# A sparse-expert encoder layer on one core: small experts in two passes with rows and rests side by side, and each weight tile split by one cast and one subtraction

## The chip, the cores and the metric

The kernel runs on one core of a Trainium2 chip. The metric is the device time of one execution in microseconds (us). Before the change the median of three runs was 1533.52 us (1529.77 to 1535.05).

## The reference, cut to what matters

One layer over 1024 tokens of width 1024: a conditioned norm, one projection into a convolution, a neighbourhood attention and a gated delta-rule mixer, an output projection, a second norm, and then a mixture of 32 experts (4 groups of 8, two experts per token). All of it is float32. The change lies in the experts:

```python
def expert_block(args):
    xb, e = args
    return (jax.nn.silu(xb @ w1[e]) * (xb @ w3[e])) @ w2[e]
```

Each expert has `w1` and `w3` of 1024 x 512 and `w2` of 512 x 1024. The result is scaled by the token's gate and added to the token. There are 2048 (token, expert) pairs; how many fall on an expert depends on the router.

## The kernel before, in words

The mixers and the router come first and end at about 870 us. From then on the kernel goes through 32 positions, one expert each (L1546). Positions 0 to 2 hold experts 0 to 2; the others hold the remaining experts by size, found by `by_size` (L1294) on the chip. `column(p)` (L1204) maps a position to a column of that order: positions 18 and 24 hold the two largest (columns 3 and 4), the rest follow in order of size. `ROOM` (L30) gives the rows kept for a column: 128 for the first three, 192 for the two largest, and then 128, 96, 80, 64 and 48. A room of 192 makes two blocks, one of 128 rows and a rest of 64 (`late`, L1548). A loop at L1611 runs once for every 128 rows that did not find room; its instructions are not in this trace.

**One expert.** The weights of an expert are six tiles of 1 MB, 128 partitions x 4 x 512 float32: two of `w1`, two of `w3`, two of `w2`. SP loads them (`load_tile`, L1175) into 16 buffers (`WA` 5, `WX` 3, `WB` 8, L1161); `weights` (L1528) takes the oldest and asks for the next, and a load waits for the one four before it (`FLY`, L1162). TensorE multiplies in a rounded format (F32R), so a float32 operand is cut into a rounded part and a rest: `split` (L60) casts on ScalarE (`wh`) and subtracts on VectorE (`wl`). `chunk_split` (L1268) cuts a weight tile into two halves of 1024 columns, each with its own `wh` and `wl`, from a pool `exw` of three buffers each (L1266). The first four tiles are split in pieces of 512.

**One block** (`class Block`, L1359). `gather` fetches the rows, `x` transposes them (eight transposes, L1378) and splits them into `xh` and `xl`. `hidden` (L1504) makes `h1` and `h3`: for each of four weight tiles, `mm3` (L1351) multiplies three passes, (`xh`,`wh`), (`xl`,`wh`), (`xh`,`wl`), with the rows as the stationary operand and 512 weight columns moving: 12 matmuls per tile, whatever the number of rows. `gated` (L1382) makes `u` = silu(h1) * h3, `t` (L1389) transposes `u` (four transposes) and splits it into `uh` and `ul`, and `y` (L1399) makes the output from two tiles in three passes and scales it into `yo`; `out` adds `yo` to the residual by an indirect DMA.

**Order.** In the program position p does: `hidden(p)`, `x` of the block of p + 1, `output(p - 1)`, `t(p)`. The weight tiles are used strictly in that order. The order on each engine is made from it when the kernel is built; each engine then works through its own list in order, and semaphores hold it where a buffer or an operand is missing. A buffer of a pool goes to the next tile when the last instruction that uses the old one has ended.

The last two blocks are not scattered; their rows are added to the residual on the chip (`last`, L1584), which ends in the final norm and the stores.

Of the kernel before, what the change touches and what calls it, by code (L numbers as in the profile page):

```python
# [16 lines left out]
P = 128  # L17
# [3 lines left out]
KT = D // P  # L21
# [5 lines left out]
TWICE = (18, 24)  # L27
LATE = 5
FEATS = (*range(0, 1280, P), *range(1536, 3072, P))
ROOM = ((3, 128), (5, 192), (12, 128), (16, 96), (20, 80), (27, 64), (32, 48))  # L30


def body(tc, I, O):
# [5 lines left out]
def _body(ctx, tc, nc, I, O):  # L39
# [1118 lines left out]
        yield  # L1158

    VS = 2  # L1160
    WA, WX, WB = 5, 3, 8  # L1161
    FLY = 4  # L1162
    arrived = mybir.DependencyInfo(mybir.DependencyClass.Sync, mybir.DependencyReason.DATA)
    loaded, used, loads, flying = [], [0], [0], []
# [98 lines left out]
        dve.tensor_scalar(v, tv, 0.0, 1e6, op0=OP.is_equal, op1=OP.mult)  # L1263
        dve.scalar_tensor_tensor(ix_, tv, -1.0, v, op0=OP.add, op1=OP.add)

    exw = ctx.enter_context(tc.tile_pool(name="exw", bufs=3))  # L1266

    def chunk_split(w, n=1):  # L1268

        parts = []  # L1270
        for k0 in (0, 2):
            wh = exw.tile([P, 2, 512], F32R, name="wh")
            wl = exw.tile([P, 2, 512], F32R, name="wl")
            for k in range(0, 2, 2 // n):
                split(*(x[:, k:k + 2 // n] for x in (wh, wl, w[:, k0:k0 + 2])))
            parts.append((wh, wl))
        return parts

    indices(mo, tab[:, 0], ix, E)
    gp = tab[:, 1]  # L1280
# [70 lines left out]
    def mm3(out, xh, xl, k0, w, first, last):  # L1351
        n = 0
        for k in range(4):
            wh, wl = w[k // 2]
            for a, b in ((xh, wh), (xl, wh), (xh, wl)):
                pe.matmul(out, a[:, k0 + k], b[:, k % 2], start=first and n == 0, stop=last and n == 11)  # L1356
                n += 1

    class Block:  # L1359


        def __init__(self, i, idx, n=P):
            self.n = n
            self.xg, self.idx, self.yo = xgs[i % 3][:n], lambda: [x[:n] for x in idx()], None

        def gather(self):
            return pool.indirect_dma_start(out=self.xg, out_offset=None, in_=xn_d,  # L1367
# [2 lines left out]

        def x(self):
            n = self.n
            xh = ex.tile([P, KT, P], F32R, name="xh")[:, :, :n]
            xl = ex.tile([P, KT, P], F32R, name="xl")[:, :, :n]
            for g in range(2):
                pt = pse.tile([P, 4, P], F32, name="pt", bufs=2)[:, :, :n]
                for j in range(4):
                    pe.transpose(pt[:, j], self.xg[:, (4 * g + j) * P:(4 * g + j + 1) * P], ident[:n, :n])  # L1378
                split(xh[:, 4 * g:4 * g + 4], xl[:, 4 * g:4 * g + 4], pt)
            self.xs = xh, xl  # L1380

        def gated(self, n):  # L1382
            if n:
                self.yo = ex.tile([P, D], F32, name="yo", bufs=2)[:self.n]
            u = self.u = self.yo[:, :512] if n else ex.tile([P, 512], F32, name="u", bufs=1)[:self.n]
            act.activation(u, self.hs[0], AF.Silu)
            dve.tensor_mul(u, self.hs[1], u)

        def t(self, n=0):  # L1389
            m = self.n  # L1390
            pt = pse.tile([P, 4, P], F32, name="ut")[:, :, :m]
            for j in range(4):
                pe.transpose(pt[:, j], self.u[:, j * P:(j + 1) * P], ident[:m, :m])
            uh = ex.tile([P, 4, P >> n], F32R, name=f"uh{n}", bufs=1)[:, :, :m]
            ul = ex.tile([P, 4, P >> n], F32R, name=f"ul{n}", bufs=1)[:, :, :m]
            split(uh, ul, pt)
            self.us = uh, ul
# [41 lines left out]
    def slots_of(ebs, ob):  # L1439


        m = len(ebs)
        pb = ex.tile([P, 2, NT], F32, name="pb", bufs=1)
        dve.tensor_scalar(pb, pos, ob, None, op0=OP.add)
        sl = ex.tile([P, NT, 2, 2, 2], F32, name="sl", bufs=1)[:, :, :, :m]
        on = ex.tile([P, NT, 2], F32, name="on", bufs=1)
        for i, eb in enumerate(ebs):
            dve.tensor_scalar(on, eid, eb, None, op0=OP.is_equal)
            dve.tensor_mul(sl[:, :, :, i], slot, on[:, :, :, None].to_broadcast([P, NT, 2, 2]))
        tabo = pse.tile([P, 512], F32, name="tab")[:, :2 * m]  # L1450
        n = 0
        for t in range(NT):
            for a in range(2):
                q = ex.tile([P, P], F32, name="q", bufs=1)
                dve.tensor_scalar(q, iota, pb[:, a, t:t + 1], None, op0=OP.is_equal)
                pe.matmul(tabo, q, sl[:, t, a].rearrange("p i k -> p (i k)"), start=n == 0, stop=n == 2 * NT - 1)
                n += 1
        tb = small.tile([P, 2, 2], F32, name="tb")[:, :m]
        dve.tensor_copy(tb, tabo.rearrange("p (i k) -> p i k", k=2))
        ix1 = small.tile([P, 2], I32, name="ix1")[:, :m]  # L1460
        indices(small, tb[:, :, 0], ix1, m)
        return [(ix1[:, i:i + 1], tb[:, i, 1:2], tb[:, i, 0:1]) for i in range(m)]
# [41 lines left out]
    def hidden(bs, weights, between=iter(())):  # L1504

        for b in bs:
            b.hs = []
        for nms in (("h1", "tab"), ("h3", "y")):
            for b, nm in zip(bs, nms):
                b.hs.append(pse.tile([P, 512], F32, name=nm, bufs=2 if nm == "y" else 1)[:b.n])  # L1510
            for g in range(2):
                next(between, None)
                w = weights()
                for b in bs:
                    mm3(b.hs[-1], *b.xs, 4 * g, w, g == 0, g == 1)
        for n, b in enumerate(bs):
            b.gated(n)

# [7 lines left out]
                b.out()  # L1526

    def weights():  # L1528
        w = chunk_split(loaded.pop(0), 2 if used[0] < 4 else 1)
        used[0] += 1  # L1530
        owed[0] += 1
        while owed[0] and len(loaded) + used[0] < len(loading) and (
# [346 lines left out]
```

## Time and profile before

| | |
|---|---|
| median of the runs | 1533.52 us |
| the profiled execution, its own time | 1529.12 us |
| its span (first to last instruction) | 1527.3 us |
| mean granted TensorE clock | 0.967 |
| TensorE matmul busy | 1380.7 us (90%) |
| VectorE busy | 1185.0 us (78%) |
| ScalarE busy | 792.4 us (52%) |
| GpSimd busy | 380.9 us (25%) |
| largest DMA queue | 351.13 MB |

Line numbers (L61) are those of the kernel before. PE is TensorE's matmuls, PEld its weight loads, DVE VectorE, ACT ScalarE, POOL GpSimd, SP the engine that issues most DMAs. A group is named by its line, its engine and its operands, output first: `h<-wh,xl` is a matmul into `h` with `wh` moving and `xl` stationary. Busy time of the matmuls counts overlapped ones once; their ends are modelled. A clock of 1.00 is 2.4 GHz.

### The profile page before, as it was taken

How to read it: one execution, taken by the hardware profiler on the slowest of the kernel's cores; microseconds unless marked ns; L12 is line 12 of the kernel's file. 1: busy time of each engine (PE TensorE's matmuls, PEld its weight loads, DVE VectorE, ACT ScalarE, POOL GpSimd, SP SyncE). 2: the span in 40 equal slices, each digit the busy share in tenths (PEclk: the TensorE clock that was granted, in tenths of full speed). 3: DMA queues.
4: the chain of work that ended last, by engine and by line, in shares of the span. 5: the costliest groups of instructions: out<-in, count | busy, mean ns of one | idle time of the engine just before them, and what ended most of it. 6: DMA issues, size and time to landing. Idle time of an engine off the chain costs nothing. (4 is left out here: it accounts for less than half of the span.)

```text
span 1527.3 us, 21968 instructions
## 1 busy us (share of the span) xinstructions
PE 1380.7 (90%) x7319; PEld 1054.2 (69%) x7319; DVE 1185.0 (78%) x2148; ACT 792.4 (52%) x1293; POOL 380.9 (25%) x294
## 2 busy tenths in 40 slices
PE   3987999999877898879999699999999999999994
PEld 3865777777665888878887578787766665665542
DVE  6758766554647688867788799999999789878995
ACT  3633554433444322322322288787777567657773
POOL 0011321100101555633432111221244113212222
PEclk9999999999999999999999599999999999999997
DMA  9496455224778665677566699999999999979832
GB/s 338 120 200 195 143 183 165 88 75 96 204 208 208 187 202 181 203 252 238 207 207 226 255 335 374 346 381 364 351 374 370 363 337 371 334 271 339 322 111 117
DMA packets 172601, 375.75 MB, mean 246 GB/s; under 512 B 33458, under 2 KB 99634, under 8 KB 147908
## 3 DMA queue, kind: packets, MB, share of 16 engines
q1 hardware_dynamic: 162500, 351.13, 67.2%
q0 software_dynamic: 7072, 16.73, 4.6%
q10 hardware_dynamic: 2912, 6.46, 1.4%
q8 instruction: 59, 0.97, 0.3%
q14 instruction: 58, 0.48, 0.1%
HBM read 325.31 MB, written 56.87 MB: 250 GB/s over the span
## 5 line engine op out<-in xcount | busy, mean ns | idle before, releaser
L61 DVE TENSOR_TENSOR wl<-w,wh 128x1024 fp32r<-128x1024 f32 (+1 forms) x392 | 460.6, 1196 | 44.8 <-ACT wh L61 39.7
L61 ACT CAST wh<-w 128x1024 fp32r<-128x1024 f32 (+1 forms) x392 | 403.9, 1033 | 161.2 <-PE y L1356 69.1
L1356 PE MATMUL h<-wl,xh 128*128 128x512 f32 (+4 forms) x512 | 204.1, 399 | 0.4 <-DVE wl L61 0.3
L1356 PE MATMUL h<-wh,xh 128*128 128x512 f32 (+4 forms) x512 | 204.4, 399 | 0.1
L1356 PE MATMUL h<-wh,xl 128*128 128x512 f32 (+4 forms) x512 | 202.0, 394 | 0.6 <-DVE xl L61 0.6
L1408 POOL DMA_INDIRECT x_d<-yo,ixp x27 | 100.0, 3703 | 198.6 <-DVE yo L1404 184.1
L339 PE MATMUL mm<-hh,wh 128*128 128x512 f32 x352 | 148.1, 421 | 0.0
L339 PE MATMUL mm<-hh,wl 128*128 128x512 f32 x352 | 143.0, 406 | 1.9 <-DVE wl L61 1.9
L339 PE MATMUL mm<-hl,wh 128*128 128x512 f32 x352 | 142.6, 405 | 0.0
L1356 PE MATMUL y<-wh,uh 128*128 128x512 f32 (+4 forms) x272 | 108.8, 401 | 1.1 <-ACT uh L61 1.1
L1356 PE MATMUL y<-wl,uh 128*128 128x512 f32 (+4 forms) x272 | 108.1, 398 | 0.1
L1356 PE MATMUL y<-wh,ul 128*128 128x512 f32 (+4 forms) x272 | 106.9, 394 | 0.5 <-DVE ul L61 0.5
L1356 PEld LDWEIGHTS h<-wl,xh 128*128 128x128 f32 (+4 forms) x512 | 80.9, 158 | 36.8 <-DVE wl L61 2.0
L1356 PEld LDWEIGHTS h<-wh,xl 128*128 128x128 f32 (+4 forms) x512 | 81.0, 158 | 36.7 <-DVE xl L61 1.4
L1356 PEld LDWEIGHTS h<-wh,xh 128*128 128x128 f32 (+4 forms) x512 | 81.1, 158 | 34.2 <-ACT wh L61 0.7
L1367 POOL DMA_INDIRECT oacc<-xn_d,ixp x29 | 35.2, 1213 | 211.4 <-PE pt L1378 195.5
L339 PEld LDWEIGHTS mm<-hh,wh 128*128 128x128 f32 x352 | 68.1, 193 | 18.5 <-issue 7.0
L339 PEld LDWEIGHTS mm<-hl,wh 128*128 128x128 f32 x352 | 67.7, 192 | 15.5 <-issue 0.3
L339 PEld LDWEIGHTS mm<-hh,wl 128*128 128x128 f32 x352 | 68.1, 193 | 13.9 <-DVE wl L61 2.2
L404 POOL TENSOR_TENSOR acc<-acc,wa 128x512 f32<-128x512 f32 x28 | 41.1, 1466 | 86.3 <-ACT wa L402 47.8
L1356 PEld LDWEIGHTS y<-wl,uh 128*128 128x128 f32 (+4 forms) x272 | 42.5, 156 | 21.2 <-DVE wl L61 2.2
L1356 PEld LDWEIGHTS y<-wh,uh 128*128 128x128 f32 (+4 forms) x272 | 42.4, 156 | 19.4 <-ACT uh L61 1.6
(433 smaller groups left out, 2893.3 us busy)
## 6 DMA issues: line engine op xcount, KB each, us to landing
w<-we SPq DMA_DIRECT2D x192, 1024.0 KB
wa<-w_ada SPq DMA_DIRECT2D x64, 256.0 KB
wa<-w_ada SPq DMA_DIRECT2D x16, 512.0 KB
wr<-w_in_f SPq DMA_DIRECT2D x16, 512.0 KB
qkv_d<-t SPq DMA_DIRECT2D x12, 512.0 KB
f<-qkv_d SPq DMA_DIRECT2D x8, 768.0 KB
t_d<-zt SPq DMA_DIRECT2D x8, 516.0 KB
xt<-x SPq DMA_DIRECT2D x8, 512.0 KB
```

The source lines that it names most:

```text
L61: return act.copy(hi, src), dve.tensor_sub(lo, src, hi.bitcast(F32))
L339: pe.matmul(ps, a[:, k], of(b, k, h * 512, 512), start=n == 0, stop=n == 3 * KT - 1)
L404: pool.tensor_add(acc, acc, w)
L1356: pe.matmul(out, a[:, k0 + k], b[:, k % 2], start=first and n == 0, stop=last and n == 11)
L1367: return pool.indirect_dma_start(out=self.xg, out_offset=None, in_=xn_d, in_offset=bass.IndirectOffsetOnAxis(ap=self.idx()[0], axis=0), bo ...
L1408: return pool.indirect_dma_start(out=x2_d, out_offset=bass.IndirectOffsetOnAxis(ap=self.idx()[0], axis=0), in_=self.yo, in_offset=None, bo ...
```

## The change

Small experts (a room of 64 or less) put the rounded rows and their rests side by side in one stationary operand of 128 columns, so that two passes (`wh`, `wl`) do for the hidden part: partitions 0 to 63 of `h` hold the products of the rounded rows, 64 to 127 those of the rests. A matrix `fold` (two identities of 64) then adds the two halves while it transposes; Silu and the product follow after the transposition. The output keeps three passes. `ROOM` has two sizes behind the two largest experts, 128 up to column 13 and 64 from there on. `chunk_split` splits a whole tile by one cast and one subtraction, into two buffers in place of three half ones; the first four tiles still go in pieces of 512. The weight tiles have 15 buffers in place of 16. The scratch `q` of `slots_of` uses the buffer of `u`.

```diff
--- before.py
+++ after.py
@@ -27,7 +27,8 @@
 TWICE = (18, 24)
 LATE = 5
 FEATS = (*range(0, 1280, P), *range(1536, 3072, P))
-ROOM = ((3, 128), (5, 192), (12, 128), (16, 96), (20, 80), (27, 64), (32, 48))
+ROOM = ((3, 128), (5, 192), (14, 128), (32, 64))
+HALF = P // 2
 
 
 def body(tc, I, O):
@@ -1158,7 +1159,7 @@
         yield
 
     VS = 2
-    WA, WX, WB = 5, 3, 8
+    WA, WX, WB = 4, 3, 8
     FLY = 4
     arrived = mybir.DependencyInfo(mybir.DependencyClass.Sync, mybir.DependencyReason.DATA)
     loaded, used, loads, flying = [], [0], [0], []
@@ -1263,18 +1264,15 @@
         dve.tensor_scalar(v, tv, 0.0, 1e6, op0=OP.is_equal, op1=OP.mult)
         dve.scalar_tensor_tensor(ix_, tv, -1.0, v, op0=OP.add, op1=OP.add)
 
-    exw = ctx.enter_context(tc.tile_pool(name="exw", bufs=3))
+    exw = ctx.enter_context(tc.tile_pool(name="exw", bufs=2))
 
     def chunk_split(w, n=1):
 
-        parts = []
-        for k0 in (0, 2):
-            wh = exw.tile([P, 2, 512], F32R, name="wh")
-            wl = exw.tile([P, 2, 512], F32R, name="wl")
-            for k in range(0, 2, 2 // n):
-                split(*(x[:, k:k + 2 // n] for x in (wh, wl, w[:, k0:k0 + 2])))
-            parts.append((wh, wl))
-        return parts
+        wh = exw.tile([P, 4, 512], F32R, name="wh")
+        wl = exw.tile([P, 4, 512], F32R, name="wl")
+        for k in range(0, 4, 4 // n):
+            split(*(x[:, k:k + 4 // n] for x in (wh, wl, w)))
+        return [(wh[:, k:k + 2], wl[:, k:k + 2]) for k in (0, 2)]
 
     indices(mo, tab[:, 0], ix, E)
     gp = tab[:, 1]
@@ -1356,12 +1354,25 @@
                 pe.matmul(out, a[:, k0 + k], b[:, k % 2], start=first and n == 0, stop=last and n == 11)
                 n += 1
 
+    fold = ex.tile([P, HALF], F32, name="fold", bufs=1)
+    dve.tensor_add(fold, ident[:, :HALF], ident[:, HALF:])
+
+    def mm2(out, xs, k0, w, first, last):
+
+        n = 0
+        for k in range(4):
+            for b in w[k // 2]:
+                pe.matmul(out, xs[:, k0 + k], b[:, k % 2], start=first and n == 0, stop=last and n == 7)
+                n += 1
+
     class Block:
+
 
 
         def __init__(self, i, idx, n=P):
             self.n = n
             self.xg, self.idx, self.yo = xgs[i % 3][:n], lambda: [x[:n] for x in idx()], None
+            self.both = n <= HALF
 
         def gather(self):
             return pool.indirect_dma_start(out=self.xg, out_offset=None, in_=xn_d,
@@ -1370,16 +1381,28 @@
 
         def x(self):
             n = self.n
-            xh = ex.tile([P, KT, P], F32R, name="xh")[:, :, :n]
-            xl = ex.tile([P, KT, P], F32R, name="xl")[:, :, :n]
+            xh = ex.tile([P, KT, P], F32R, name="xh")
+            if self.both:
+                self.xs = xh
+                xh, xl = xh[:, :, :n], xh[:, :, HALF:HALF + n]
+            else:
+                xh, xl = xh[:, :, :n], ex.tile([P, KT, P], F32R, name="xl")[:, :, :n]
+                self.xs = xh, xl
             for g in range(2):
                 pt = pse.tile([P, 4, P], F32, name="pt", bufs=2)[:, :, :n]
                 for j in range(4):
                     pe.transpose(pt[:, j], self.xg[:, (4 * g + j) * P:(4 * g + j + 1) * P], ident[:n, :n])
                 split(xh[:, 4 * g:4 * g + 4], xl[:, 4 * g:4 * g + 4], pt)
-            self.xs = xh, xl
+
+        def hidden(self, w, g):
+            (mm2 if self.both else mm3)(self.hs[-1], *((self.xs,) if self.both else self.xs), 4 * g, w, g == 0, g == 1)
 
         def gated(self, n):
+            if self.both:
+                self.hc = ex.tile([P, KT, P], F32, name="xl").rearrange("p (i k) f -> p i k f", i=2)
+                for i in range(2):
+                    act.copy(self.hc[:, i].rearrange("p k f -> p (k f)"), self.hs[i])
+                return
             if n:
                 self.yo = ex.tile([P, D], F32, name="yo", bufs=2)[:self.n]
             u = self.u = self.yo[:, :512] if n else ex.tile([P, 512], F32, name="u", bufs=1)[:self.n]
@@ -1388,9 +1411,20 @@
 
         def t(self, n=0):
             m = self.n
-            pt = pse.tile([P, 4, P], F32, name="ut")[:, :, :m]
-            for j in range(4):
-                pe.transpose(pt[:, j], self.u[:, j * P:(j + 1) * P], ident[:m, :m])
+            pt = pse.tile([P, 4, P], F32, name="ut")
+            if self.both:
+                ht = pt.rearrange("p k (i f) -> p i k f", i=2)
+                for i in range(2):
+                    for j in range(4):
+                        pe.matmul(ht[:, i, j], self.hc[:, i, j], fold, start=True, stop=True)
+                su = ex.tile([P, 512], F32, name="u", bufs=1).rearrange("p (i k f) -> p i k f", i=2, k=4)
+                act.activation(su[:, 0], ht[:, 0], AF.Silu)
+                dve.tensor_mul(su[:, 1], ht[:, 1], su[:, 0])
+                pt = su[:, 1][:, :, :m]
+            else:
+                pt = pt[:, :, :m]
+                for j in range(4):
+                    pe.transpose(pt[:, j], self.u[:, j * P:(j + 1) * P], ident[:m, :m])
             uh = ex.tile([P, 4, P >> n], F32R, name=f"uh{n}", bufs=1)[:, :, :m]
             ul = ex.tile([P, 4, P >> n], F32R, name=f"ul{n}", bufs=1)[:, :, :m]
             split(uh, ul, pt)
@@ -1451,7 +1485,7 @@
         n = 0
         for t in range(NT):
             for a in range(2):
-                q = ex.tile([P, P], F32, name="q", bufs=1)
+                q = ex.tile([P, 512], F32, name="u", bufs=1)[:, :P]
                 dve.tensor_scalar(q, iota, pb[:, a, t:t + 1], None, op0=OP.is_equal)
                 pe.matmul(tabo, q, sl[:, t, a].rearrange("p i k -> p (i k)"), start=n == 0, stop=n == 2 * NT - 1)
                 n += 1
@@ -1507,12 +1541,12 @@
             b.hs = []
         for nms in (("h1", "tab"), ("h3", "y")):
             for b, nm in zip(bs, nms):
-                b.hs.append(pse.tile([P, 512], F32, name=nm, bufs=2 if nm == "y" else 1)[:b.n])
+                b.hs.append(pse.tile([P, 512], F32, name=nm, bufs=2 if nm == "y" else 1)[:P if b.both else b.n])
             for g in range(2):
                 next(between, None)
                 w = weights()
                 for b in bs:
-                    mm3(b.hs[-1], *b.xs, 4 * g, w, g == 0, g == 1)
+                    b.hidden(w, g)
         for n, b in enumerate(bs):
             b.gated(n)
 
@@ -1526,7 +1560,7 @@
                 b.out()
 
     def weights():
-        w = chunk_split(loaded.pop(0), 2 if used[0] < 4 else 1)
+        w = chunk_split(loaded.pop(0), 4 if used[0] < 4 else 1)
         used[0] += 1
         owed[0] += 1
         while owed[0] and len(loaded) + used[0] < len(loading) and (
```

## Rows read from the trace of the kernel before

**Rows 1.** The page: busy time of the engines, and the granted clock in 40 slices.
```profile
PE 1380.7 (90%) x7319; PEld 1054.2 (69%) x7319; DVE 1185.0 (78%) x2148; ACT 792.4 (52%) x1293; POOL 380.9 (25%) x294
...
PEclk9999999999999999999999599999999999999997
```

**Rows 2.** Busy time by windows of the expert stage; last: clock, DMA share, GB/s.
```profile
core 0: us, PE busy (x) PEld busy (x) DVE busy (x) ACT busy (x) POOL busy (x), PEclk, DMA share, GB/s
1040.00:1180.00 140.00, 139.98 (x665) 98.69 (x664) 136.60 (x143) 111.29 (x127) 43.93 (x16) 1.00 1.00 363
1380.00:1440.00 60.00, 60.00 (x276) 32.10 (x275) 54.82 (x58) 45.00 (x53) 17.59 (x6) 1.00 0.95 356
```

**Rows 3.** Waits from 880 to 1440 us: us in total, times, longest us.
```profile
ACT wh L61 <- PE y L1356: 61.5, 104, 3.2
ACT wh L61 <- PE h L1356: 59.3, 151, 1.5
```

**Rows 4.** Activations at L1386 in four windows: count, durations (ns), first and last start.
```profile
L1386 ACT ACTIVATE u<-h x11: 583/587/591, 894.3 to 1078.7; 128x512 f32<-128x512 f32 x9, 96x512 f32<-96x512 f32 x2
...
L1386 ACT ACTIVATE u<-h x7: 583/585/588, 1078.7 to 1184.9; 80x512 f32<-80x512 f32 x4, 96x512 f32<-96x512 f32 x3
...
L1386 ACT ACTIVATE u<-h x10: 582/586/597, 1184.9 to 1383.4; 64x512 f32<-64x512 f32 x7, 128x512 f32<-128x512 f32 x2, 80x512 f32<-80x512 f32 x1
...
L1386 ACT ACTIVATE u<-h x6: 579/584/587, 1383.4 to 1475.0; 48x512 f32<-48x512 f32 x5, 64x512 f32<-64x512 f32 x1
```

**Rows 5.** TensorE in order of time, 1405 to 1408 us: start, duration, instruction.
```profile
1406.23 0.40 PE L1356 MATMUL h<-wh,xh 128*48 128x512 f32 x1
1406.47 0.40 PE L1356 MATMUL h<-wh,xl 128*48 128x512 f32 x1
```

**Rows 6.** TensorE in order of time, 884 to 887 us: eight transposes.
```profile
885.31 1.03 PE L1378 MATMUL pt<-ident,oacc 128*128 128x128 f32 x8
```

**Rows 7.** Groups by form, 850 us to the end: busy us, mean ns, idle before.
```profile
L61 DVE TENSOR_TENSOR wl<-w,wh 128x1024 fp32r<-128x1024 f32 x376 | 450.0, 1218 | 43.8 <-ACT wh L61 38.9
L61 ACT CAST wh<-w 128x1024 fp32r<-128x1024 f32 x376 | 395.0, 1051 | 157.2 <-PE y L1356 69.1 <-PE h L1356 65.3 <-issue 8.0
...
L61 DVE TENSOR_TENSOR xl<-pt,xh 128x512 fp32r<-128x512 f32 x24 | 16.3, 684 | 0.8 <-ACT xh L61 0.6
...
L1404 DVE SCALAR_TENSOR_TENSOR yo<-y,tabp,oacc 128x512 f32<-128x512 f32 x18 | 13.5, 748 | 1.5 <-PE y L1356 1.4
...
L61 DVE TENSOR_TENSOR wl<-w,wh 128x512 fp32r<-128x512 f32 x16 | 10.7, 683 | 1.0 <-ACT wh L61 0.8
...
L61 DVE TENSOR_TENSOR xl<-pt,xh 128x256 fp32r<-128x256 f32 x18 | 7.0, 410 | 0.4 <-ACT xh L61 0.4
...
L61 ACT CAST wh<-w 128x512 fp32r<-128x512 f32 x16 | 8.9, 616 | 4.0 <-PE h L1356 2.8 <-PE pl L1020 1.2
```

**Rows 8.** ScalarE in order of time, around 1406 and 1490 us; idle before, and releaser.
```profile
1405.49 1.05 ACT L61 CAST wh<-w 128x1024 fp32r<-128x1024 f32 x1 [0.36 <-PE h L1356]
1406.90 1.05 ACT L61 CAST wh<-w 128x1024 fp32r<-128x1024 f32 x1 [0.36 <-PE h L1356]
...
1489.84 1.05 ACT L61 CAST wh<-w 128x1024 fp32r<-128x1024 f32 x1 [2.33 <-PE y L1356]
```

**Rows 9.** VectorE in order of time, around 1407 and 1488 us.
```profile
1406.57 1.23 DVE L61 TENSOR_TENSOR wl<-w,wh 128x1024 fp32r<-128x1024 f32 x1 [0.19 <-ACT wh L61]
...
1488.28 0.34 DVE L61 TENSOR_TENSOR ul<-ut,uh 128x192 fp32r<-128x192 f32 x1
```

**Rows 10.** TensorE in order of time, around 1489 us: a matmul that waited for a subtraction.
```profile
1488.68 0.43 PE L1356 MATMUL y<-wh,ul 128*48 128x512 f32 x1 [0.46 <-DVE ul L61]
```

**Rows 11.** SP's weight loads, 1040 to 1180 us and 1180 us on: first and last start.
```profile
L1178 SPq DMA_DIRECT2D w<-we x44: 332/333/342, 1041.9 to 1179.9; - x44
...
L1178 SPq DMA_DIRECT2D w<-we x80: 332/333/346, 1179.9 to 1441.7; - x80
```

**Rows 12.** Busy time and granted clock, 400 to 440 us (columns as in rows 2).
```profile
400.00:440.00 40.00, 31.51 (x166) 25.11 (x165) 19.73 (x41) 19.49 (x63) 5.42 (x4) 0.93 0.69 199
```

## The prediction

> **What bounds the kernel now.** I read the page first: TensorE is busy 90% of the span at a granted clock of 9 tenths or more in nearly every slice, VectorE 78% [rows 1]. These are means over different stages, and every edit lies in the expert stage (about 870 us to the end), so I took that by windows next. From 1040 to 1180 us the matmuls fill 139.98 of 140 us, VectorE 136.60, and the DMA engines 1.00 of their time [rows 2]: three resources are full together. The waits say which one ends last. The longest ones on ScalarE and VectorE are casts that wait for matmuls (`wh` waits for `y` and `h`, 255 times, 120.8 us) [rows 3]; TensorE waits for nothing of note. So TensorE sets the pace, and a cast starts when a matmul lets go of a `wh` buffer. The ScalarE activations at L1386, one per position, give the pace: position 1 to 11 take 184.4 us, 11 to 17 106.2, 17 to 26 198.5 (positions 18 and 24 have a rest beside them), 26 to 31 91.6 [rows 4]. That is 17.7 us for an undisturbed single position (106.2 / 6) and 18.3 for the last ones (91.6 / 5).
>
> **The change, part by part.**
>
> *Matmuls saved.* Matmuls of 512 columns start 0.23 to 0.24 us apart (the recorded 0.40 overlaps the next) [rows 5]; I use 0.23. A single position has 72 of them (16.6 us) and 12 transposes at 0.13 (eight take 1.03 us [rows 6]): 18.1 us at most, which is the measured pace. After, a 64-row block needs 8 instead of 12 for each of four hidden tiles, 56 in all. In 18 small positions and 2 rests that is 320 x 0.23 = 74 us less on TensorE. Whether the span gets them depends on what feeds TensorE.
>
> *Splits merged.* By form, a cast takes 616 ns for 512 elements and 1051 for 1024, a subtraction 683 and 1218 [rows 7]. The slopes, 0.85 and 1.045 ns per element, put a cast of 2048 at 1.92 us and a subtraction at 2.29; no row has this size, and the bounds are twice the short one (2.10, 2.44) and the bare slope (1.74, 2.14). Per tile VectorE saves 2 x 1.218 - 2.29 = 0.15 us, 29 us over 192 tiles.
>
> *Buffers.* This is the part that decides. Before, three half-tile slots: a slot is taken from the start of its cast to the last `wh` matmul of that half. Rows show each link: the last `wh` matmul of a half starts at 1406.47 and lasts 0.40 [rows 5], and the next cast starts at 1406.90 [rows 8], 0.03 later; the cast of 1405.49 ends at 1406.54 [rows 8] and its subtraction starts at 1406.57 [rows 9]; a subtraction that ends at 1488.62 lets its matmul go at 1488.68 [rows 9, 10], 0.06 later. From the first `wl` matmul of a half (its third) to its last `wh` matmul (its fifth) are 2 steps, so a slot turns round in 0.06 + 0.46 + 0.40 + 0.03 + 1.05 + 0.03 + 1.22 = 3.25 us, and three slots could deliver a tile (two halves) every 2.2 us; TensorE takes 2.95. Cover enough.
>
> After, two whole-tile slots. With three passes, from the third matmul to the eleventh are 8 steps: 0.06 + 1.84 + 0.40 + 0.03 + 1.92 + 0.03 + 2.29 = 6.57 us for a slot, so a tile every 3.29 us at best, though TensorE needs 2.76. With two passes the first `wl` matmul is the second and the last `wh` one the seventh, 5 steps: 5.88 us, a tile every 2.94, though TensorE needs 1.84. Each of the two slots serves three of the six tiles of a position: a 128-row position is 3 x 6.57 = 19.7 us, a small one (output keeps three passes) 2 x 5.88 + 6.57 = 18.3. The first is 2.0 us above today, and the small ones, for which the passes were cut, stay where they are: the cut passes turn into TensorE waiting for `wl`.
>
> *Positions.* The new ROOM makes positions 0 to 11 single 128-row blocks, 18 and 24 a 128-row block with a 64-row rest, and the other 18 small. Position 1 to 11: ten times 17.7 are 177 of the 184.4 us; the other 7.4 (start, and the slot lists of position 5) lie partly in the new stalls, I keep 4. So 197 + 4 = 201, +16.6; the hidden part of position 0, four tiles at up to 0.34 more (3.29 against 2.95), adds 1. Position 11 to 17: 6 x 18.33 = 110.0, +3.8. Position 17 to 26 is two groups of three intervals about a rest, and three single ones. In such a group the hidden tiles of 18 have 20 matmuls (4.6 us, over the slots' 4.2, so TensorE-bound), four of them 18.4; its output tiles, 24 matmuls each, take 11.0; the two other output pairs 6.6 each, two small hidden parts 11.8 each, and 1.5 for transposes in the bound parts: 67.7. Twice 67.7 and 3 x 18.33 are 190.4 against 198.5, -8.1. Position 26 to 31: 5 x 18.33 = 91.7, +0.1. Tail: the last splits are 4.2 us long instead of 2.3, and the chain fold, Silu, product, split before the last output has two operations more; +2, bounds 0 and +5. Together +15.4 us.
>
> *Operations that meet the chain.* A slot's turn holds only if ScalarE and VectorE are free at the moment. VectorE has, between subtractions, 3.29 - 2.29 = 1.0 us per tile, into which a position's six others must fit (`xl` 0.684 twice, `u` and `ul` of that size, `yo` 0.748 twice [rows 7]; 4.2 us, in a small position 3.1, with `xl` 0.41). One that comes ready late in the gap delays the subtraction by up to 0.4; the same holds for ScalarE's four casts and activations, and the 12 transposes (1.6 us) stand partly among the matmuls of the turn. Bounds: 0.3 us per position (all in gaps) and 2.0 (half of it in the way). I take 1.0, since before too some of them fall into VectorE's short gaps: 24 single intervals, +24 us (7 to 48).
>
> *Edits at no cost.* The fold: eight matmuls of 64 columns instead of four transposes, between 0.13 and 0.23 each, +0.5 to +1.3 us of TensorE per small position, where it now stands 18.3 - 12.9 - 1.0 = 4.4 us; without that cover, +1 us times 18. The two ScalarE copies of 128x512 replace an activation at about 0.6; ScalarE, 111.29 of 140 us busy [rows 2], keeps 1.3 us per tile. The product on VectorE shrinks from 512 columns to 256. One weight tile fewer ahead: SP issued 44 loads from 1041.9 to 1179.9, 3.21 us apart, with DMA full [rows 11, 2]. At 19.7 us per six tiles (3.29) loads keep up, so nothing; if the stage ran faster than 3.21 per tile this would be the next bound. `q` in `u`'s buffer stays one buffer as before and waits at one position, 0 to 3 us, within the 4 above.
>
> **Sum.** The profiled execution took 1529.1 us; + 15.4 + 24 = 1568.5. The median of the runs is 4.4 above the profiled one, so 1573 in their terms.
>
> **Rivals.**
> 1. *VectorE was the true limit and its relief counts.* VectorE is 97.6% busy from 1040 to 1180 [rows 2]. If waits for slots are only shadows of it, fewer operations and passes win: small positions go to VectorE's pace, 54.82 of 60 us busy [rows 2] x 18.3 = 16.7, less 0.9 for six splits and 0.3 for the product: 15.5. Then loads bound: the last is issued at 1441.7 [rows 11], at 3.21 us each from 1179.9 it would be 1433.5, landing some 13 later (four in flight), against a last cast at 1489.84 [rows 8]: -43, 1486, 1490 in the runs' terms. It decides from the point where cast and subtraction together fit beside one tile's matmuls, 3.2 us; they are 4.2. Against: TensorE itself is unbroken, and casts wait for matmuls, not for VectorE [rows 3]. The Trainium skill (Perfetto Trace Analysis, Optimizing Scalar/DVE Operations) says that larger operations raise throughput if the engine is saturated, which speaks for this rival; the same section says that breaking instructions up may finish work sooner where ScalarE and VectorE hold other engines up, which speaks for my sum. VectorE at 97.6% meets the first condition today, and the slot's turn makes the second one true after.
> 2. *The clock.* With stalls in every tile the granted clock may fall: 400 to 440 us had TensorE busy 31.51 of 40 and 0.93 granted [rows 12]. If the stage gets 0.90 (a fifth of the time at 1.2 GHz, where a step takes twice 0.23), the five steps of a turn cost 1.15 us more in that fifth, 3.5 per small position, 0.7 in the mean; the eight steps of a large one 5.5, 1.1 in the mean. 18 x 0.7 + 10 x 1.1 = 24 us: 1597.
> 3. *An expert overflows.* With rooms of 64 from column 14 on, an expert above that would run the loop at L1611. Counted from the reference on its inputs, the sizes after the first three columns, sorted, are 150, 136, 112, 107, 107, 100, 100, 96, 90, 79, 76, 58 and less: column 14 gets 58. So no.
> 4. *No difference*: all operations in gaps and the tail free, and the 16.6 of the large positions half hidden. About +5 us.
>
> **Chances.** Mine 0.80, its own range 1555 to 1598 (operations 0.3 to 2.0 per position, tail 0 to 5). Clock 0.06, the faster case 0.08, no difference 0.06. With 0.3% (4.6 us) as what a measurement can tell: faster 0.08, same 0.06, slower 0.86. For 8 in 10 the range goes from 1548 to 1600.
>
> **What would show it.** Cast 1.9 us and subtraction 2.3 by form. TensorE in the 128-row positions no longer full, with waits for `wl` of its own; positions 6 to 11 at 20 to 21 us, small ones at 18 to 20; SP waiting for buffers, not for loads. Wrong if position 1 to 11 takes under 190 us, if small positions fall below 17, or if the loads wait for each other all through.

## The result and the profile after

The kernel after takes 1582.53 us (median of four runs, 1574.84 to 1583.4) where the kernel before, on the same chip, takes 1531.83 (median of four runs, one more than at the start; 1529.77 to 1535.05): a ratio of 1.0318, with a 95% interval of 1.0279 to 1.0356. The change made the kernel 3.2% slower. The forecast was 1573, with 1548 to 1600 as its range. The profiled execution of after took 1582.37 us with a span of 1580.5, that of before 1529.12 and 1527.3, so 53.2 us of span are to be found.

The page of after: busy time, share of the span and instructions of each engine, then the granted clock in 40 slices.

```profile
PE 1373.7 (87%) x7239; PEld 1084.1 (69%) x7239; DVE 1165.5 (74%) x1955; ACT 773.2 (49%) x1145; POOL 352.2 (22%) x294
...
PEclk9999999999987999999997799999999999999997
```

Every engine is a smaller share of a longer span than in [rows 1], but for the weight loads (PEld), which stay at 69%. No engine has become the bound; they wait for each other. Busy time by windows of after (columns as in [rows 2]), the stretch of 128-row positions with the first small ones, and then a stretch of small ones alone:

```profile
1040.00:1180.00 140.00, 127.57 (x585) 95.52 (x584) 120.95 (x86) 95.14 (x75) 31.60 (x14) 1.00 1.00 352
...
1440.00:1500.00 60.00, 53.29 (x256) 36.48 (x254) 52.39 (x41) 42.92 (x39) 5.75 (x5) 1.00 0.90 328
```

Where TensorE was busy for 139.98 of 140 us [rows 2], it now has 127.57, at a clock of 1.00: it stalls, and in these windows the clock does not fall for it. VectorE goes from 136.60 to 120.95. The waits of after from 880 to 1490 us (total, times, longest, in us):

```profile
DVE wl L62 <- ACT wh L62: 93.3, 105, 3.0
ACT wh L62 <- PE h L1354: 61.9, 45, 5.2
ACT wh L62 <- PE y L1354: 60.7, 50, 3.6
...
ACT wh L62 <- PE h L1365: 51.1, 44, 2.1
PEld h L1365 <- DVE wl L62: 40.8, 44, 1.9
...
PE h L1365 <- DVE wl L62: 25.8, 33, 1.5
PEld y L1354 <- DVE wl L62: 20.8, 29, 1.4
```

This is a ring. The cast waits for the matmul to let go of the buffer, as in [rows 3], the subtraction waits for the cast, and now the matmul waits for the subtraction, which it did nowhere of note before (L62 is the split, L1354 the three-pass product, L1365 the two-pass one). Rows that close in a ring say that no single engine is short; the time is in the length of the turn. By form, the merged operations (busy us, mean ns, idle before):

```profile
L62 DVE TENSOR_TENSOR wl<-w,wh 128x2048 fp32r<-128x2048 f32 x188 | 430.9, 2292 | 97.9 <-ACT wh L62 96.2
L62 ACT CAST wh<-w 128x2048 fp32r<-128x2048 f32 x188 | 358.5, 1907 | 196.7 <-PE y L1354 66.9 <-PE h L1365 59.1 <-PE h L1354 56.2
...
L1419 PE MATMUL ut<-fold,xl 128*128 128x64 f32 x320 | 40.8, 270 | 0.0
L1404 ACT COPY xl<-h 128x512 f32<-128x512 f32 x36 | 20.8, 578 | 0.0
```

Before, cast and subtraction of half a tile took 1051 and 1218 ns [rows 7]; one of 1907 and one of 2292 are 0.20 and 0.14 us less per tile. The operations did get cheaper, and the kernel slower. One turn of a buffer in after, in order of time (start, duration, engine; idle before and releaser in brackets):

```profile
1080.69 1.91 ACT L62 CAST wh<-w 128x2048 fp32r<-128x2048 f32 x1 [1.29 <-PE h L1354]
...
1082.63 2.29 DVE L62 TENSOR_TENSOR wl<-w,wh 128x2048 fp32r<-128x2048 f32 x1 [1.40 <-ACT wh L62]
...
1084.98 0.50 PE L1354 MATMUL y<-wl,uh 128*128 128x512 f32 x1 [0.67 <-DVE wl L62]
...
1086.92 0.39 PE L1354 MATMUL y<-wh,ul 128*128 128x512 f32 x1
...
1087.35 1.91 ACT L62 CAST wh<-w 128x2048 fp32r<-128x2048 f32 x1 [0.81 <-PE y L1354]
```

Follow the buffer: cast at 1080.69, its subtraction at 1082.63, which ends at 1084.92; the first `wl` matmul of the tile at 1084.98, 0.06 later; the eleventh of its twelve matmuls, the last that reads `wh`, at 1086.92; and the next cast into this buffer at 1087.35, 0.04 after that one's end. That is 6.66 us for a turn, 3.33 per tile with two buffers, where twelve matmuls need 2.76.

The pace of positions, from the starts of one activation per position (first and last start are behind the durations): six of 128 rows (positions 6 to 11), then the six small ones from 26 to 31.

```profile
L1409 ACT ACTIVATE u<-h x6: 585/592/593, 1018.5 to 1118.8; 128x512 f32<-128x512 f32 x6
...
L1421 ACT ACTIVATE u<-ut x6: 368/376/378, 1439.8 to 1533.7; 128x256 f32<-128x256 f32 x6
```

100.3 / 5 = 20.06 us for a large position and 93.9 / 5 = 18.8 for a small one, against 17.7 and 18.3 [rows 4].

### The profile page after: what moved, and what is told of

Same layout as the page of the kernel before. It is cut to its first block, busy times and chain, and to the rows that moved or that the text cites. A ratio compares the mean times of both kernels' runs of the same rounds, so it can differ in the third digit from the quotient of the medians.

```text
span 1580.5 us, 21156 instructions
## 1 busy us (share of the span) xinstructions
PE 1373.7 (87%) x7239; PEld 1084.1 (69%) x7239; DVE 1165.5 (74%) x1955; ACT 773.2 (49%) x1145; POOL 352.2 (22%) x294
## 5 line engine op out<-in xcount | busy, mean ns | idle before, releaser
L62 DVE TENSOR_TENSOR wl<-w,wh 128x2048 fp32r<-128x2048 f32 (+1 forms) x204 | 441.5, 2166 | 101.0 <-ACT wh L62 99.2
L62 ACT CAST wh<-w 128x2048 fp32r<-128x2048 f32 (+1 forms) x204 | 367.2, 1805 | 203.6 <-PE y L1354 66.9
L1365 PE MATMUL h<-wl,xh 128*128 128x512 f32 x288 | 119.7, 417 | 31.7 <-DVE wl L62 31.1
L1354 PE MATMUL y<-wl,uh 128*64 128x512 f32 (+1 forms) x272 | 111.3, 411 | 10.5 <-DVE wl L62 10.4
L1365 PE MATMUL h<-wh,xh 128*128 128x512 f32 x288 | 114.3, 397 | 4.1 <-ACT wh L62 4.1
L1354 PE MATMUL y<-wh,uh 128*64 128x512 f32 (+1 forms) x272 | 107.9, 397 | 2.3 <-ACT uh L62 2.1
L1354 PE MATMUL y<-wh,ul 128*64 128x512 f32 (+1 forms) x272 | 107.8, 396 | 1.5 <-DVE ul L62 1.5
L1354 PE MATMUL h<-wl,xh 128*128 128x512 f32 x224 | 93.9, 419 | 3.8 <-DVE wl L62 3.8
L1365 PEld LDWEIGHTS h<-wl,xh 128*128 128x128 f32 x288 | 54.1, 188 | 59.1 <-DVE wl L62 48.9
L1354 PE MATMUL h<-wh,xh 128*128 128x512 f32 x224 | 91.2, 407 | 0.8 <-ACT xh L62 0.7
L1354 PE MATMUL h<-wh,xl 128*128 128x512 f32 x224 | 90.0, 402 | 0.9 <-DVE xl L62 0.9
L340 PEld LDWEIGHTS mm<-hh,wh 128*128 128x128 f32 x352 | 68.6, 195 | 18.6 <-issue 7.2
L1354 PEld LDWEIGHTS y<-wl,uh 128*64 128x64 f32 (+1 forms) x272 | 42.9, 158 | 39.5 <-DVE wl L62 22.9
L1365 PEld LDWEIGHTS h<-wh,xh 128*128 128x128 f32 x288 | 54.2, 188 | 15.0 <-ACT wh L62 4.7
```

Source lines behind the costliest of these rows:

```text
L62: return act.copy(hi, src), dve.tensor_sub(lo, src, hi.bitcast(F32))
L340: pe.matmul(ps, a[:, k], of(b, k, h * 512, 512), start=n == 0, stop=n == 3 * KT - 1)
L1365: pe.matmul(out, xs[:, k0 + k], b[:, k % 2], start=first and n == 0, stop=last and n == 7)
```

## The experiments

Ratios are to the kernel before, run on the same chip. The first two take the two parts of the change by themselves, and the others take one suspected cost each.

**The split alone.** The kernel before with the merged split, two whole-tile buffers and one tile fewer ahead; the rooms and the three passes are those of before.

```diff
-    WA, WX, WB = 5, 3, 8
+    WA, WX, WB = 4, 3, 8
-    exw = ctx.enter_context(tc.tile_pool(name="exw", bufs=3))
+    exw = ctx.enter_context(tc.tile_pool(name="exw", bufs=2))
...
+        wh = exw.tile([P, 4, 512], F32R, name="wh")
+        wl = exw.tile([P, 4, 512], F32R, name="wl")
```

> The merged split alone: one cast and one subtraction per tile, two whole-tile buffers, 15 weight buffers; three passes for all and the rooms as before. Slot theory: every single position at 3 x 6.57 us + what the changed kernel shows on top, 20.05; positions 18 and 24 with their rests stay TensorE-bound. 12 positions + 2.3, 16 + 1.8, start and tail + 10: 1590 to 1610, slower than the whole change. Rival (VectorE's relief counts, the passes' fold is what costs): at or below 1532.

It took 1595.84 us, 1.0423 [1.0396, 1.045]. Its activations (line 1383 here), positions 6 to 11 and 26 to 31:

```profile
L1383 ACT ACTIVATE u<-h x6: 579/588/595, 1005.8 to 1106.8; 128x512 f32<-128x512 f32 x4, 96x512 f32<-96x512 f32 x2
...
L1383 ACT ACTIVATE u<-h x6: 586/588/592, 1441.0 to 1540.3; 48x512 f32<-48x512 f32 x5, 64x512 f32<-64x512 f32 x1
```

20.2 us and 19.9 us a position, both near the 20.06 of the large positions of after: with three passes everywhere, small positions too run at the turn of the two buffers. The loss is the split's (with its two buffers), and it is larger than that of the whole change.

**The passes alone.** The kernel after with the three half-tile buffers, the halved split and the tiles ahead of before; the new rooms, the fold and `q` in `u`'s buffer stay.

```diff
-    WA, WX, WB = 4, 3, 8
+    WA, WX, WB = 5, 3, 8
-    exw = ctx.enter_context(tc.tile_pool(name="exw", bufs=2))
+    exw = ctx.enter_context(tc.tile_pool(name="exw", bufs=3))
...
+        for k0 in (0, 2):
+            wh = exw.tile([P, 2, 512], F32R, name="wh")
+            wl = exw.tile([P, 2, 512], F32R, name="wl")
```

> The small experts' two passes, the fold and the new rooms alone; half-tile splits, three half buffers and 16 weight buffers as before. Slot theory: a half's slot turns in at most 3.25 us, a tile every 2.2: 128-row positions 17.7, small ones at VectorE's pace of about 16 until the weight tiles in store are used up, then at the loads' pace of 3.0 to 3.2 us per tile; 1485 to 1505. Rival (the two passes with their fold cost the time): at or above 1560.

It took 1512.93 us, 0.9883 [0.9858, 0.9909]: this part alone makes the kernel 1.2% faster, though less than the 1485 to 1505 that was expected. Against the 1529.09 of before in that batch, the split alone is +66.8 us and the passes alone -16.2; their sum is +50.6, and the whole change is 1582.53 - 1531.83 = +50.7. The two parts add up, as well as intervals of some 4 us each can tell. The small positions of the passes alone, and their window:

```profile
L1424 ACT ACTIVATE u<-ut x6: 383/385/385, 1383.9 to 1469.7; 128x256 f32<-128x256 f32 x6
```
```profile
1380.00:1440.00 60.00, 57.07 (x272) 37.55 (x270) 56.18 (x63) 49.07 (x64) 28.89 (x5) 1.00 0.91 344
```

85.8 / 5 = 17.2 us each, with VectorE at 56.18 of 60 us and TensorE at 57.07: of the saved matmuls only a part comes through. That VectorE is what holds the rest back is not shown, as TensorE is as full, and the loads waited 204.3 us for loads from 880 to 1450 us.

**The buffers of after, split in two pieces.** The same two whole-tile buffers and the same tiles ahead, but two casts and two subtractions of 1024 columns per tile, so that the first matmuls wait for half a subtraction, and the next cast for half a tile's matmuls.

```diff
-        w = chunk_split(loaded.pop(0), 4 if used[0] < 4 else 1)
+        w = chunk_split(loaded.pop(0), 4 if used[0] < 4 else 2)
```

> The changed kernel with each whole-tile buffer filled by two casts and two subtractions of 1024 columns; buffers, passes and rooms as changed. Slot theory: the first half's subtraction frees TensorE after 1.05 + 1.22 us, so a slot of a three-pass tile turns round in 0.06 + 1.84 + 0.40 + 0.03 + 1.05 + 0.03 + 1.22 = 4.6 us and two slots give a tile every 2.3 us, under TensorE's 2.76: 128-row positions back at 17.7 to 18.2 us (20.05 in the changed kernel), small ones at 15.5 to 17 (18.8), the whole below the kernel before, 1485 to 1510. Rival, that the two buffers in themselves or the fold and its ScalarE copies hold the stage: 128-row positions stay near 20 and small ones near 18.8, 1575 to 1585, or a little above for 29 us more VectorE time.

It took 1513.37 us, 0.9879 [0.9848, 0.991]. One number in one line turns 3.2% slower into 1.2% faster, though each tile then has 0.34 us more of work on ScalarE and VectorE. Its activations and window:

```profile
L1409 ACT ACTIVATE u<-h x6: 581/588/591, 1000.0 to 1089.6; 128x512 f32<-128x512 f32 x6
...
L1421 ACT ACTIVATE u<-ut x6: 384/386/386, 1386.7 to 1470.3; 128x256 f32<-128x256 f32 x6
```
```profile
1380.00:1440.00 60.00, 58.41 (x281) 38.76 (x280) 56.94 (x65) 48.79 (x65) 30.88 (x6) 1.00 0.97 360
```

17.9 us for a large position, 16.7 for a small one, both as expected; the total is 3 us above the expected range. Buffers and tiles ahead are those of after, so neither their size nor their number alone makes the loss: with operations half as long it is gone. The next two experiments keep the long operations and take the turn another way. SP's own waits from 880 to 1450 us:

```profile
SPq L1179 <- DMA w<-we: 216.7, 105, 4.5
SPq L1179 <- DVE wl L62: 171.2, 88, 5.2
```

Loads wait for loads again, much as in before (197.4 us for loads and 221.5 for `wl` in the same window); in after, from 1040 to 1180 us, SP waited 109.9 us for subtractions and 0.2 for loads.

```profile
SPq L1179 <- DVE wl L62: 109.9, 41, 3.3
...
SPq L1179 <- DMA w<-we: 0.2, 1, 0.2
```

**A third whole-tile buffer.** The split stays one cast and one subtraction; the third buffer's room is taken from the tiles ahead.

```diff
-    WA, WX, WB = 4, 3, 8
+    WA, WX, WB = 2, 3, 8
-    exw = ctx.enter_context(tc.tile_pool(name="exw", bufs=2))
+    exw = ctx.enter_context(tc.tile_pool(name="exw", bufs=3))
```

> The changed kernel with three whole-tile buffers for wh and wl in place of two, and 13 weight buffers in place of 15 to make room. Slot theory: 6.57 us for a slot, three of them, a tile every 2.2 us: 128-row positions back at 17.7 to 18.2 us with casts of 1.9 and subtractions of 2.3 us unchanged, small ones 16.8 to 17.8; 1505 to 1530. Rival (long instructions as such hold TensorE up): 128-row positions near 20, 1575 to 1585. Second rival (weight tiles ahead decide): with 13 the loads run out in the 128-row positions and ScalarE waits for them.

It took 1528.44 us, 0.9989 [0.9969, 1.0009]. Its activations in three stretches (positions 6 to 11, the first small ones, positions 26 to 31):

```profile
L1409 ACT ACTIVATE u<-h x6: 583/588/596, 1003.0 to 1089.6; 128x512 f32<-128x512 f32 x6
...
L1421 ACT ACTIVATE u<-ut x4: 371/372/377, 1133.8 to 1183.2; 128x256 f32<-128x256 f32 x4
...
L1421 ACT ACTIVATE u<-ut x6: 383/389/390, 1385.8 to 1479.6; 128x256 f32<-128x256 f32 x6
```

17.3 us for a large position and 16.5 for the first small ones: with three buffers a turn no longer sets the pace, with the same long operations. (Position 6, where `u` waits 7.9 us for the matmul that reads `q`, took 32.3 us from its first cast to the next position's.) But from 1385.8 it is 18.8. What stalls there shows in the order of time: the copy of `h` stands on ScalarE ahead of the next casts and waits for the matmuls, and the casts come behind it. The first line is the last matmul that reads the buffer of the first of these casts.

```profile
1426.97 0.39 PE L1365 MATMUL h<-wh,xh 128*128 128x512 f32 x1
...
1430.50 0.58 ACT L1404 COPY xl<-h 128x512 f32<-128x512 f32 x1 [3.54 <-PE h L1365]
1430.99 3.71 ACT L62 CAST wh<-w 128x2048 fp32r<-128x2048 f32 x2
```

Two casts back to back behind a wait of 3.54 us: a buffer lay free from 1427.36 and was not filled before 1430.99. From 1300 to 1470 us such copies waited 26.7 us, in 9 waits. The fewer tiles ahead do not show as a wait: from 860 us to the end the casts waited hardly at all for a load.

```profile
ACT wh L62 <- DMA w<-we: 0.9, 2, 0.8
```

Why the copy stalls the late small positions and not the first ones is not shown.

**All `wh` passes of a tile first.** The buffers and the split of after; only the order of the matmuls within a tile changes (below for three passes; the two passes likewise), so that the subtraction runs beside the `wh` matmuls and the `wh` buffer is let go before the last four.

```diff
-        for k in range(4):
-            wh, wl = w[k // 2]
-            for a, b in ((xh, wh), (xl, wh), (xh, wl)):
-                pe.matmul(out, a[:, k0 + k], b[:, k % 2], ...)
+        for k, a, i in [(k, a, 0) for k in range(4) for a in (xh, xl)] + [(k, xh, 1) for k in range(4)]:
+            pe.matmul(out, a[:, k0 + k], w[k // 2][i][:, k % 2], ...)
```

> The changed kernel with only the order of a tile's matmuls changed: all passes over wh first, then those over wl, so that the last wh matmul no longer stands behind the wait for wl. Slot theory: with cast and subtraction of 4.2 us still whole, three tiles take 1.84 + 0.69 + 4.73 = 7.3 us (2.4 per tile, three passes) or 6.3 (2.1, two passes), under TensorE's 2.76 and VectorE's 2.6 per tile: 128-row positions 17.7 to 18.2, small ones 15.5 to 17, 1485 to 1510. Rival (long instructions as such, or too few buffers as such): no change, 1575 to 1585.

It took 1522.71 us, 0.9953 [0.993, 0.9976]. The large positions of its profile:

```profile
L1407 ACT ACTIVATE u<-h x6: 578/586/596, 1004.7 to 1091.4; 128x512 f32<-128x512 f32 x6
```

17.3 us against 20.06, with the same instructions of the same lengths. The subtraction now runs beside the tile's eight `wh` matmuls and no longer between the second and the third. The total is above the 1485 to 1510 expected and gains less than the two pieces do; one place where it stays behind is position 6 (29.6 us from its first cast to the next position's), where `u` waits for the matmul that reads `q` in the same buffer:

```profile
995.25 0.60 ACT L1407 ACTIVATE u<-h 128x512 f32<-128x512 f32 x1 [7.47 <-PE tab L1488]
```

**Its own buffer for `q`.** The change put `q`, the mask of the slot lists, into the single buffer of `u`. Here it has one of its own, and its room is made by the size ranking's `pm`, which moves into an existing buffer.

```diff
-                q = ex.tile([P, 512], F32, name="u", bufs=1)[:, :P]
+                q = ex.tile([P, P], F32, name="q", bufs=1)
```

> The changed kernel with the one-hot scratch q of the slot lists in a buffer of its own again (a 32-column scratch of the size ranking gives up its place for it). Theory: in the changed kernel the activation into u of position 5 waits until the slot lists are done, because q holds u's only buffer, and position 6 comes 7 us late (27.4 us against 20.05); with its own buffer that interval is 20 to 22 and the time 1573 to 1578, about 7 us less than the changed kernel. Rival (the slot lists are late because each of their steps waits behind 2.29 us subtractions, whichever buffer they use): no change, 1580 to 1585.

It took 1572.92 us, 1.0303 [1.0266, 1.034]. The activations from position 3 to 6, where the slot lists are built, first of after, then of this kernel:

```profile
L1409 ACT ACTIVATE u<-h x4: 590/592/597, 949.1 to 1018.5; 128x512 f32<-128x512 f32 x4
```
```profile
L1409 ACT ACTIVATE u<-h x4: 584/588/595, 940.1 to 1001.5; 128x512 f32<-128x512 f32 x4
```

69.4 us against 61.4 (and 58.7 before, by the same activations). The profile shows 8 us gone from this stretch. Against before in its own batch the kernel is 44.0 us slower, where after was 50.7, but the ratio's interval overlaps that of after, so the runs do not show the gain in the total for certain. In after the stretch holds this stall, ScalarE's `u` behind the matmul that reads `q`:

```profile
1008.46 0.60 ACT L1409 ACTIVATE u<-h 128x512 f32<-128x512 f32 x1 [3.48 <-PE tab L1490]
```

**One tile fewer ahead.** The kernel before with that alone.

```diff
-    WA, WX, WB = 5, 3, 8
+    WA, WX, WB = 4, 3, 8
```

> The kernel before with 15 weight buffers in place of 16 and nothing else. Theory: the store of tiles never runs out, so nothing: 1527 to 1535. Rival (one tile fewer ahead costs the 128-row positions, where the DMA engines are full): 3 to 10 us more.

It took 1532.5 us, 1.0037 [1.002, 1.0054]. Nearly nothing, but not nothing. From position 1 on its profile has the pace of before; position 0 takes 25.1 us instead of 22.0 (first cast to first cast). SP's waits from 840 to 900 us, first of before, then of this kernel:

```profile
SPq L1178 <- DVE wl L61: 20.7, 7, 4.6
```
```profile
SPq L1178 <- DVE wl L61: 35.6, 7, 20.5
```

With one buffer fewer SP stands once for 20.5 us behind a subtraction, and from 860 to 890 us the DMA engines are busy for 0.50 of their time instead of 0.61. That this is what makes position 0 longer is not shown: from 840 to 900 us no cast waits for a load in either profile, the granted clock from 860 to 890 is 0.70 instead of 0.75, and the first cast itself starts 1.0 us earlier.

**Combinations.** The passes alone with `q` in its own buffer, the `wh` passes first with the last tiles in pieces, and the `wh` passes first with every tile in pieces (the last two with `q` in its own buffer too).

> The two passes, fold and new rooms with the split of the kernel before (half tiles, three buffers, 16 weight buffers) and q in a buffer of its own. Theory: as the run of the passes alone, 1513, less 2 to 3 us at the slot lists, where it took 20.9 and 20.8 us for two positions: 1508 to 1513. Rival (the slot lists cost what they cost): 1513.

> The changed kernel with all wh matmuls of a tile first, q in a buffer of its own, and the last 18 tiles split in two pieces. Slot theory, from the run with wh first (1522.7): its position 6 took 29.6 us against 17.7, which the buffer of its own takes back to 18 to 20, about -10; its last three intervals were 19 to 20 and its tail 68.7 us against 60.3 to 60.9 where tiles go in two pieces, about -8; 1503 to 1512. Rival (what one place gives is taken up by VectorE's or the loads' limit): 1513 or above.

> The same order of matmuls and q's own buffer, with every tile split in two pieces. Slot theory: neither slots nor the order bind; VectorE then works at its own limit, 12 subtractions at 1.13 us and 2.8 us of others, 16.4 us per small position and 17.7 (TensorE) per large one, tail 60 us: 1503 to 1512, as the run in two pieces less the slot lists. Rival (VectorE is held by the six more operations): not below the run in two pieces, 1513.

They took 1512.86 us (0.9894 [0.9862, 0.9927]), 1515.09 (0.9892 [0.9863, 0.9921]) and 1515.21 (0.9882 [0.9843, 0.9921]). None is beyond the passes alone or the two pieces: five kernels lie within 2.4 us of each other at 1.1 to 1.2% faster than before. The own buffer for `q`, which gave 8 us of profile in after, gives nothing that the runs show where the split is in halves. The two kernels with `wh` first stayed above the 1503 to 1512 expected of them. What limits all five was not taken apart further; the rows of two of them show VectorE at 56.2 and 56.9 of 60 us in the small positions, and those of the two pieces loads that wait for loads.

## Why the prediction was right, point by point

The mechanism, that two whole-tile buffers turn too slowly for TensorE, is what the runs show: with shorter operations, a third buffer or another order of matmuls the loss goes. The total came out 10 us above the forecast, and it is nearer than its parts: one term was about 13 us too large and others together about 27 too small, so that how near the sum came is in part luck. The pace of the positions is not: 20.06 and 18.8 us against 19.7 + 1.0 and 18.3 + 1.0. The steps against the two profiles, each stretch from the first weight cast of one position to that of another:

| stretch | predicted | measured |
|---|---|---|
| before the expert stage | 0 | +6.8 |
| position 0 | +1 | +3.8 |
| 1 to 11 | +16.6 + 10 = +26.6 | +28.2 |
| 11 to 17 | +3.8 + 6 = +9.8 | +7.8 |
| 17 to 26 | -8.1 + 3 = -5.1 | -0.6 |
| 26 to 31 | +0.1 + 5 = +5.1 | +2.0 |
| position 31 and the tail | +2 | +5.2 |
| sum | +39.4 | +53.2 |

The forecast counted before by activations, 198.5 us from position 17 to 26 and 91.6 from 26 to 31; by casts these are 196.1 and 94.3, so two rows of the table hold 2 to 3 us that are only the change of mark. The ends that the forecast gave to its own range, 1555 and 1598, are 1 to 2 us inside what its bounds add up to (1554 and 1600); nothing hangs on it.

*The turn of a buffer*: forecast 6.57 us, read as 6.66 in the turn above. The terms held: 1.92 and 2.29 for operations that before never ran were 1.907 and 2.292. From a cast to the next but one, positions 27 to 29 of after took 6.03 us in the mean for a hidden tile and 6.69 for an output tile, where 5.88 and 6.57 were forecast. The length of one operation was taken by itself in the two pieces: 17.9 us per large position against 20.06 on the same buffers.

*The Trainium skill* (Perfetto Trace Analysis, Optimizing Scalar/DVE Operations) has two rules that point opposite ways here. It says that grouping into larger operations can improve throughput in a saturated engine. VectorE stood at 97.6% [rows 2], and the split alone lost 4.2%. It says that breaking instructions up may finish work sooner where ScalarE and VectorE cause bubbles elsewhere, and it ties this to engines that are not saturated, which the forecast left out. VectorE was at 86% in after, TensorE stalled, and the two pieces went from 1.0318 to 0.9879. In this case the second one decided.

*Operations that meet the chain* was the term that was mis-sized: 1.0 us per position forecast, and 20.06 - 19.7 = 0.4 for a large one and 18.8 - 18.3 = 0.5 for a small one measured. Over 24 intervals that is about 13 us too much. It lay near the lower bound of 0.3, as if most of these operations found gaps of VectorE, which waited for casts for 93.3 us; that they did was not followed one by one.

*What made up for it*: the groups with a rest beside a position took 70.4 us (26.0, 23.4, 21.0) instead of 67.7, twice; position 1 and the slot lists took 13.0 us above ten times 20.06 where 4 had been kept, of which `q` in `u`'s buffer is about 8; the tail cost 5.2, just over its upper bound. Position 0 and the time before the stage, below, are the rest. In the tail the long operations show as in the steady part: position 31 to the end took 67.4 to 68.6 us in the five kernels whose tiles are all split whole and 60.3 to 63.5 in the seven that split the last tiles in halves.

*The fold* was put at +0.5 to +1.3 us of TensorE per small position. Its eight matmuls stand as 16 rows, 40.8 / 20 = 2.0 us per block, where four transposes take about 0.5 (eight take 1.03 [rows 6]); that is +1.5, above the bound, but under the stalls of after.

*One tile fewer ahead* was costed at nothing. With that alone position 0 took 3.1 us more, against 3.8 in the whole change: the cover named, that loads keep up, holds once the stage runs. At its start other things differ too. In after the granted clock was 0.50, 0.84 and 0.92 in the three stretches of 20 us from 860 to 920, where before had 0.62, 1.00 and 1.00; how much of position 0, and of position 1 (23.4 us), is the clock's was not separated.

*The 6.8 us before the stage stay open.* The start of the first weight cast varied from 860.2 to 868.0 over the profiles, and it was late in kernels that are fast (866.1 in the two pieces). The runs do not show that the change is the cause, nor that it is not.

*The rivals.* VectorE as the true limit is refuted for after (VectorE fell from 97.6% to 86% of 140 us and the kernel got slower), but it may be the bound behind the next one: with the turn gone, the small positions ran at 16.7 to 17.2 us with VectorE at 94 to 95% and TensorE at 95 to 97%, where the rival had 15.5. The clock is refuted for the steady stage, where it was 1.00 in both windows above; at the start of the stage it was lower, as said. No expert overflowed: the 188 whole casts and the four tiles in pieces are 192 tiles, six for each of 32 experts, and a run of the loop would have split more. No difference is refuted by the interval.

Of the marks that were to show it wrong, none came: positions 1 to 11 took 213.6 us, no small position of after fell below 17, and loads waited 0.2 us for loads from 1040 to 1180.

## What to carry to other kernels

Merging two operations into one saves their overhead on the engine, but it lengthens the turn of every buffer that passes through them; add the turn up, matmuls included, divide by the number of buffers, and compare with what the consumer needs per tile before merging. When every engine waits for another in a ring and none is full, shorten the turn: halve the operation, add a buffer, or reorder the consumer so that the first operands are let go early; each of the three gave back 51 to 66 us here, each against before in its own batch. Make two edits of one change separately: here one was worth 16 us and the other cost 67.

## What was not expected of the hardware

TensorE's granted clock stayed at 1.00 from 1040 to 1180 us although it stalled in every tile (127.57 of 140 us busy); at 0.93 in [rows 12] it was busy 31.51 of 40. Shared scratch showed its price only beside whole-tile splits: the same shared buffer for `q` held ScalarE for 3.48 us in after and for 7.47 us in the kernel with the `wh` passes first, but for 1.0 in the two pieces, and its removal changed nothing in the passes alone (1512.93 and 1512.86 us). Why it differs so was not looked into. And an added copy on ScalarE left a free buffer empty: it waited 3.54 us for matmuls with two casts behind it that then ran without a wait of their own.
